# Streaming-encoder trunk, float32 on one core: in the last quarter of both MLPs, the weights of the last product split ahead of those of the last but one

## Chip, core and metric

The kernel runs on one core of a Trainium2 chip. Its time is what the device needs for one execution, in microseconds, as the median over several executions. Before the change three executions took 1416.71, 1417.35 and 1418.65 us, so the median is 1417.35 us.

## What is computed

The trunk has two residual layers over 512 tokens of width 1024. The first mixes tokens with a Mamba-2 scan, the second with stick-breaking attention. Each mixer is followed by a LayerNorm, then by an MLP with a squared ReLU, then by another LayerNorm:

```python
D_MODEL, SEQ, DEPTH, D_FF = 1024, 512, 2, 4096
DEEPNORM_ALPHA = (2 * DEPTH) ** 0.25

def squared_relu_mlp(h, w1, w2):
    return jnp.square(jax.nn.relu(h @ w1)) @ w2
...
    for layer in range(DEPTH):
        if layer < N_A_LAYERS:
            mix = mamba2_mixer(h, ...)
        else:
            if layer == N_A_LAYERS:
                k, v = shared_kv(h, sb_w_k, sb_w_v)
            mix = stick_breaking_attention(h, sb_w_q[j], k, v, sb_w_o[j])
        h = layer_norm(DEEPNORM_ALPHA * h + mix, ln_mix_g[layer], ln_mix_b[layer])
        h = layer_norm(DEEPNORM_ALPHA * h + squared_relu_mlp(h, mlp_w1[layer], mlp_w2[layer]),
                       ln_mlp_g[layer], ln_mlp_b[layer])
    return h
```

Only the two MLPs, and what follows each of them, concern the change. After the first MLP come its LayerNorm and the projections to v, q and k. After the second come its LayerNorm and the output.

## The kernel before

**Precision.** Every operand of a matrix product is split in two: a high part (a cast of the value, on ScalarE, named `wh` for weights) and a low part (the value less its high part, mostly on VectorE, named `wl`). A product is then three matmuls (`mm3`, lines 208 to 210): high with high, and the two mixed ones.

**Weights.** All weights come through one list, `stream`, in pieces of 128x1024 (512 KB). `emit_w` (from line 150) handles the next piece: SyncE's queue loads it into one of two `raw` buffers (`wr`), ScalarE casts the high part (line 191), VectorE subtracts for the low part (line 193). The split pair takes a buffer from a ring of six in the MLPs (four in `wp`, two in the MLP's own pool). `load_w` hands a piece to its product and keeps splitting up to four pieces ahead (`prefetch`). Since there are two `raw` buffers, the load of a piece can begin only when the low part of the piece two places before it has been formed.

**The MLP's second matrix.** It is applied in four quarters of the hidden width, each as a 2x2 block product with seven products instead of eight, P1 to P7. Four of them need a sum or difference of weight blocks, kept in buffers `rawa` and `rawc` (two of each, one for each half `s` of a piece pair): `t1` leaves its sum in `rawa`, `t2` in `rawc`, and `t3` and `t4` read `rawc`. The order of the products is P1, P5, P6, P4, P7, P2, P3, each with two pieces of weights and 24 matmuls of 512 columns. They gather in four pairs of PSUM banks: X (P1, P6, P7), Y (P5, then P3), Z (P4), V (P2). VectorE adds a finished pair onto the residual `v`: line 435 for a plain add, line 432 for an add that also leaves the row sums that the norm needs (`ln_sums`). "Row 2" is token tiles 0 and 1, "row 1" is token tiles 2 and 3.

**The last quarter.** P7 finishes row 2, which can then be normalised: sums (line 343), squares on ScalarE (346), 1/sqrt on GpSimd (348 to 354), shift (359) and scale (365) on VectorE. P2 (banks V, left half of the columns) and P3 (banks Y, right half) finish row 1. In the first MLP the normed rows are transposed on TensorE into banks `ln_b` (396), copied out as `ln_hh` (399) and `ln_hl` (400), and used by the projections `pv`, `pq` and `pk`, first for row 2 and then for row 1. In the second MLP the normed rows are written out (367).

**What sets the order.** The code is recorded in program order, and a scheduler then places the instructions of each engine by its own estimate. `issue_after` (in the first MLP for P2, P3 and what follows, in `by_token` for the second) only bounds where something may be placed. So the order on an engine follows from when the scheduler expects the operands, the split weights among them. Once the program is built, each engine runs its instructions in that fixed order.

Of the kernel before, what the change touches and what calls it, by code (L numbers as in the profile page):

```python
# [12 lines left out]
F32R = mybir.dt.float32r  # L13
# [4 lines left out]
P = 128  # L18
# [17 lines left out]
def trunk(ctx: ExitStack, tc: tile.TileContext, io):  # L36
    nc = tc.nc
# [16 lines left out]
    def f(x):  # L54
        return x.bitcast(F32)
# [28 lines left out]
    stream = []  # L84
    marks = []
# [56 lines left out]
    ready = []  # L142
# [2 lines left out]
    alt = {}  # L145
    upto = [len(stream)]
    sums = {}
    depth = [2]

    def emit_w():  # L150
        i = len(ready)
        pool, e = extra[:2]
        if i >= extra[4]:
            pool = None
        use = pool is not None and e > 0 and i % (4 + e) >= 4
        px, b = (pool, e) if use else (wp, 4)
        sfx = "x" if use else ""
        rb = extra[2]

        def fetch(src, tag=None):  # L160
            if tag is not None:
                raw = pool.tile([P, 1024], F32, tag=tag, name=f"{tag}{i}", bufs=2)
            elif pool is not None and i % (2 + rb) >= 2:
                raw = pool.tile([P, 1024], F32, tag="rawx", name=f"wr{i}", bufs=rb)
            else:
                raw = wp.tile([P, 1024], F32, tag="raw", name=f"wr{i}", bufs=2)
            nc.sync.dma_start(raw, src)
            return raw

        item = stream[i]  # L170
        if not isinstance(item, tuple):
            raw = fetch(item)
        elif item[0] == "t1":
            raw = sums[item[1]] = fetch(item[2], "rawa")
            nc.vector.tensor_sub(raw, raw, fetch(item[3]))
        elif item[0] == "t2":
            raw = fetch(item[2], "rawc")
            nc.vector.tensor_sub(raw, raw, sums[item[1]])
            sums[item[1]] = raw
        else:  # L180
            raw = fetch(item[2])
            if item[0] == "t3":
                nc.vector.tensor_sub(raw, sums[item[1]], raw)
            else:
                nc.vector.tensor_sub(raw, raw, sums[item[1]])
        if i in alt:
            hi, lo = alt[i](i)
        else:
            hi = px.tile([P, 1024], F32R, tag="hi" + sfx, name=f"wh{i}", bufs=b)
            lo = px.tile([P, 1024], F32R, tag="lo" + sfx, name=f"wl{i}", bufs=b)  # L190
        nc.scalar.copy(hi, raw)  # L191
        eng = nc.gpsimd if extra[3] and i % 4 == 1 else nc.vector
        eng.tensor_sub(lo, raw, f(hi))  # L193
        ready.append((hi, lo))

    def prefetch(n):
        while len(ready) < min(upto[0], taken[0] + n):
            emit_w()
# [1104 lines left out]
```

## Time and profile before

| what | value |
|---|---|
| median of three executions | 1417.35 us |
| the profiled execution's own time | 1416.35 us |
| its span | 1414.2 us |
| mean granted TensorE clock | 0.997 |
| busy TensorE matmul / weight load | 1389.0 us / 1197.0 us |
| busy VectorE / ScalarE / GpSimd | 1076.8 / 783.8 / 221.8 us |
| HBM read / written | 159.65 MB / 2.10 MB |

The span is the stretch from the first to the last event in the trace; 2.15 us of the profiled execution's time lie outside it. A row of the timeline gives the start, the duration, the engine, the line and operation, what is written and read, and in brackets how long the engine was idle before and what ended that. Matmuls overlap in the pipeline: one of 512 columns is shown with 0.39 us and the next begins 0.227 us later. Neighbouring rows on VectorE overlap a little too, so the cost of an instruction in a row of busy ones is the distance between starts.

### The profile page before, as it was taken

The page shows a single profiled execution, that of the slowest core. Times are in us where ns is not written, and L with a number is a line of the kernel's source. Part 1 is how long each engine was busy: PE and PEld are TensorE (multiplying, and loading weights), DVE is VectorE, ACT ScalarE, POOL GpSimd, SP SyncE. Part 2 cuts the span into 40 slices and gives each one's busy share as a digit, 9 for nine tenths or more (in the row PEclk, how much of TensorE's full clock was granted, in tenths as well). Part 3 has the DMA queues.
Part 4 walks back from the last instruction along what each step waited for, and adds up shares of the span by engine and source line. Part 5 has one row for each costly group of instructions (what it writes and reads, how often), then busy time and mean ns, then how long its engine had stood idle before and what let it go on. Part 6 is the DMA issues. An engine that isn't in the chain of part 4 may idle for free.

```text
span 1414.2 us, 19327 instructions
## 1 busy us (share of the span) xinstructions
PE 1389.0 (98%) x7414; PEld 1197.0 (85%) x7414; DVE 1076.8 (76%) x1530; ACT 783.8 (55%) x1264; POOL 221.8 (16%) x249
## 2 busy tenths in 40 slices
PE   9999999999999999999999999999999999999996
PEld 6898897889997988888888799899889888888885
DVE  5798898368887596785859868787877966858588
ACT  5556575246653363635445568898853636454463
POOL 2344555034443100000000200000000000000001
PEclk9999999999999999999999999999999999999998
DMA  5223222222223345455453521121223455454533
GB/s 186 76 77 133 70 66 75 89 81 70 74 65 107 115 162 169 159 162 166 134 169 116 163 90 47 44 75 46 75 90 120 134 179 164 149 168 139 168 116 123
DMA packets 46699, 162.99 MB, mean 115 GB/s; under 512 B 5520, under 2 KB 5776, under 8 KB 46608
## 3 DMA queue, kind: packets, MB, share of 16 engines
q1 hardware_dynamic: 44016, 157.44, 34.9%
q10 hardware_dynamic: 2592, 4.33, 1.0%
q8 instruction: 58, 0.95, 0.3%
q14 instruction: 33, 0.27, 0.1%
HBM read 159.65 MB, written 2.10 MB: 114 GB/s over the span
## 4 chain that ended last, share of the span: by engine, by line
PE 87%; DVE 7%; ACT 2%; DMA 2%; issue 1%; POOL 1%; ACTq 0%; SPq 0%; DVEq 0%; POOLq 0%
PE f L209 8%; PE f L210 8%; PE f L208 8%; PE X L210 3%; PE X L208 3%; PE X L209 3%; PE pz L208 2%; PE pz L210 2%; PE pz L209 2%; PE px L208 2%; PE px L209 2%; PE px L210 2%; PE Y L210 2%; PE Y L209 2%; PE Y L208 2%; PE z L1141 1%
## 5 line engine op out<-in xcount | busy, mean ns | idle before, releaser
L191 ACT CAST wh<-wr 128x1024 fp32r<-128x1024 f32 x235 | 246.6, 1050 | 326.1 <-DMA wr<-w 159.1
L193 DVE TENSOR_TENSOR wl<-wr,wh 128x1024 fp32r<-128x1024 f32 x218 | 268.6, 1233 | 181.6 <-ACT wh L191 180.8
L210 PE MATMUL f<-ln_hh,wl 128*128 128x512 f32 (+1 forms) x544 | 201.2, 371 | 0.0
L209 PE MATMUL f<-ln_hl,wh 128*128 128x512 f32 (+1 forms) x544 | 201.2, 371 | 0.0
L208 PE MATMUL f<-ln_hh,wh 128*128 128x512 f32 (+1 forms) x544 | 200.3, 371 | 0.0
L210 PEld LDWEIGHTS f<-ln_hh,wl 128*128 128x128 f32 x544 | 102.4, 188 | 17.8 <-DVE wl L193 0.4
L209 PEld LDWEIGHTS f<-ln_hl,wh 128*128 128x128 f32 x544 | 102.4, 188 | 17.7 <-DVE ln_hl L400 0.2
L208 PEld LDWEIGHTS f<-ln_hh,wh 128*128 128x128 f32 x544 | 102.0, 188 | 17.4
L348 POOL TENSOR_TENSOR ln_rs<-ln_sums 128x1 f32<-128x1 f32 (+1 forms) x6 | 3.1, 513 | 632.6 <-ACT lnr L346 632.6
L208 PE MATMUL X<-wh,hP 128*128 128x512 f32 x192 | 74.7, 389 | 0.0
L209 PE MATMUL X<-wl,hP 128*128 128x512 f32 x192 | 74.7, 389 | 0.0
L210 PE MATMUL X<-wh,l 128*128 128x512 f32 x192 | 74.0, 389 | 0.0
L210 PE MATMUL pz<-wh,x_l 128*128 128x256 f32 x256 | 72.7, 284 | 0.0
L209 PE MATMUL pz<-wl,x_h 128*128 128x256 f32 x256 | 72.6, 284 | 0.0
L208 PE MATMUL pz<-wh,x_h 128*128 128x256 f32 x256 | 72.4, 283 | 0.0
L461 ACT CAST hP<-r 128x512 fp32r<-128x512 f32 x80 | 48.1, 620 | 32.0 <-DVE r L473 31.1
L193 POOL TENSOR_TENSOR wl<-wr,wh 128x1024 fp32r<-128x1024 f32 x17 | 42.6, 2504 | 92.3 <-ACT wh L191 92.0
L208 PE MATMUL px<-x_h,wh 128*128 128x512 f32 x128 | 50.8, 397 | 0.0
L209 PE MATMUL px<-x_l,wh 128*128 128x512 f32 x128 | 50.3, 393 | 0.0
L210 PE MATMUL px<-x_h,wl 128*128 128x512 f32 x128 | 50.2, 392 | 0.0
L209 PE MATMUL Y<-wl,hP 128*128 128x512 f32 x128 | 49.8, 389 | 0.0
L209 PEld LDWEIGHTS pz<-wl,x_h 128*128 128x128 f32 x256 | 48.8, 190 | 0.9
(1365 smaller groups left out, 3923.0 us busy)
## 6 DMA issues: line engine op xcount, KB each, us to landing
wr<-w SPq DMA_DIRECT2D x160, 512.0 KB, 3.6
wr<-w_bc SPq DMA_DIRECT2D x16, 512.0 KB, 3.5
wr<-w_x SPq DMA_DIRECT2D x16, 512.0 KB, 3.5
wr<-w_z SPq DMA_DIRECT2D x16, 512.0 KB, 3.5
wr<-w_so SPq DMA_DIRECT2D x16, 512.0 KB, 3.5
rawa<-w SPq DMA_DIRECT2D x16, 512.0 KB, 3.7
rawc<-w SPq DMA_DIRECT2D x16, 512.0 KB, 4.4
wr<-w_qk SPq DMA_DIRECT2D x16, 512.0 KB, 3.5
```

Source lines behind the costliest of these rows:

```text
L191: nc.scalar.copy(hi, raw)
L193: eng.tensor_sub(lo, raw, f(hi))
L208: nc.tensor.matmul(out, a[0], b[0], start=start, stop=False, skip_group_check=skip)
L209: nc.tensor.matmul(out, a[0], b[1], start=False, stop=False, skip_group_check=skip)
L210: return nc.tensor.matmul(out, a[1], b[0], start=False, stop=stop, skip_group_check=skip)
L348: nc.gpsimd.tensor_add(rs, self.sq[:, t0:t1, 0], self.sq[:, t0:t1, 1])
L461: nc.scalar.copy(h, src)
L1141: w_end[0] = nc.tensor.matmul(zj, ntri_ge, x, start=False, stop=i == 1, skip_group_check=True).ins
```

## The change

Where the second piece of P7 has been split (`i in last_t3`, five places before the end of each MLP's stream), the two pieces of P3 (places `i + 3` and `i + 4`) are now loaded and split at once, ahead of the two of P2. Their high and low parts go to four tiles with the tags `rawc` and `rawa`, whose buffers held the sums of weight blocks. When `emit_w` later comes to those places, it takes the kept pair and issues nothing. No instruction is added or left out.

```diff
+    spare = {}
+    last_t3 = (marks[1] - 5, marks[3] - 5)
...
     def emit_w():
         i = len(ready)
+        if i in spare:
+            ready.append(spare[i])
+            return
...
         eng.tensor_sub(lo, raw, f(hi))
         ready.append((hi, lo))
+        if i in last_t3:
+            for n, tag in ((i + 3, "rawc"), (i + 4, "rawa")):
+                hi, lo = (pool.tile([P, 1024], F32R, tag=tag, name=f"{tag}{n}{j}", bufs=2) for j in "hl")
+                raw = fetch(stream[n])
+                nc.scalar.copy(hi, raw)
+                nc.vector.tensor_sub(lo, raw, f(hi))
+                spare[n] = (hi, lo)
```

The lines of the changed file are 12 higher below this place (208 becomes 220, 432 becomes 444). The order on the engines moves at three places. In the rows, V with a number is one half of P2's bank pair, Y with a number one half of P3's, `ln_b` with a number one bank of transposes.

VectorE at the end of the first MLP, before, from the sums of row 2 to the first low part of the transposed rows:

```order
L343 TENSOR_SCALAR ln_sums<-ln_sums 128x1
L193 TENSOR_TENSOR wl_7366<-wr_7363,wh_7365 128x1024
L359 SCALAR_TENSOR_TENSOR v<-v,ln_sums,lnr_7308 128x1024
L432 SCALAR_TENSOR_TENSOR v,ln_sums<-v,V_7391 128x512
L432 SCALAR_TENSOR_TENSOR v,ln_sums<-v,V_7392 128x512
L359 SCALAR_TENSOR_TENSOR v<-v,ln_sums,lnr_7308 128x1024
L365 SCALAR_TENSOR_TENSOR v<-v,ln_rs,lnr_7308 128x1024 x2
L193 TENSOR_TENSOR wl_7409<-wr_7406,wh_7408 128x1024
L432 SCALAR_TENSOR_TENSOR v,ln_sums<-v,Y_7226 128x512
L432 SCALAR_TENSOR_TENSOR v,ln_sums<-v,Y_7227 128x512
L193 TENSOR_TENSOR wl_7497<-wr_7494,wh_7496 128x1024
L400 TENSOR_TENSOR ln_hl<-ln_b_7452,ln_hh 128x2x256
```

The same stretch of VectorE in the changed kernel:

```order
L355 TENSOR_SCALAR ln_sums<-ln_sums 128x1
L198 TENSOR_TENSOR wl_7346<-wr_7343,wh_7345 128x1024
L371 SCALAR_TENSOR_TENSOR v<-v,ln_sums,lnr_7320 128x1024 x2
L377 SCALAR_TENSOR_TENSOR v<-v,ln_rs,lnr_7320 128x1024 x2
L198 TENSOR_TENSOR wl_7409<-wr_7406,wh_7408 128x1024
L444 SCALAR_TENSOR_TENSOR v,ln_sums<-v,Y_7226 128x512
L444 SCALAR_TENSOR_TENSOR v,ln_sums<-v,Y_7227 128x512
L198 TENSOR_TENSOR wl_7497<-wr_7494,wh_7496 128x1024
L444 SCALAR_TENSOR_TENSOR v,ln_sums<-v,V_7391 128x512
L444 SCALAR_TENSOR_TENSOR v,ln_sums<-v,V_7392 128x512
L412 TENSOR_TENSOR ln_hl<-ln_b_7452,ln_hh 128x2x256
```

The two adds of V stood between the two shifts of row 2. They now stand behind the second weight piece of `pv` (`wl_7497`), directly ahead of the first `ln_hl`.

TensorE near the end of the second MLP, before, where the first matmuls of P2 stand (`wh_12836` is P2's first piece, `wh_12809` P7's second, X_12703 one half of P7's banks):

```order
L208 MATMUL X_12703<-wh_12809,hP_12386 128x512
L208 MATMUL V_12936<-wh_12836,hP_12387 128x512
L208 MATMUL V_12937<-wh_12836,hP_12387 128x512
L209 MATMUL X_12703<-wl_12810,hP_12386 128x512
L210 MATMUL X_12703<-wh_12809,l_12382 128x512
```

In the changed kernel the first matmuls of P2 stand here (`rawa271h` and `rawa271l` are P3's second piece, `wh_12848` is P2's first):

```order
L222 MATMUL Y_12745<-rawc270h,lP_12390 128x512
L220 MATMUL Y_12745<-rawa271h,hP_12389 128x512
L220 MATMUL V_12936<-wh_12848,hP_12387 128x512
L220 MATMUL V_12937<-wh_12848,hP_12387 128x512
L221 MATMUL Y_12745<-rawa271l,hP_12389 128x512
```

P2 stood inside P7 and ran ahead of the whole of P3. Now P3 stands first, and P2 begins in the middle of P3's first half (Y_12745) and ends last.

VectorE at the end of the program, before, from P3's adds to the last scales:

```order
L432 SCALAR_TENSOR_TENSOR v,ln_sums<-v,Y_12745 128x512
L365 SCALAR_TENSOR_TENSOR v<-v,ln_rs,lnr_12827 128x512
L343 TENSOR_SCALAR ln_sums<-ln_sums 128x1
L432 SCALAR_TENSOR_TENSOR v,ln_sums<-v,Y_12746 128x512
L343 TENSOR_SCALAR ln_sums<-ln_sums 128x1
L359 SCALAR_TENSOR_TENSOR v<-v,ln_sums,lnr_12827 128x512 x3
L365 SCALAR_TENSOR_TENSOR v<-v,ln_rs,lnr_12827 128x512 x2
```

The same stretch in the changed kernel:

```order
L377 SCALAR_TENSOR_TENSOR v<-v,ln_rs,lnr_12839 128x512 x3
L444 SCALAR_TENSOR_TENSOR v,ln_sums<-v,Y_12746 128x512
L444 SCALAR_TENSOR_TENSOR v,ln_sums<-v,V_12936 128x512
L444 SCALAR_TENSOR_TENSOR v,ln_sums<-v,V_12937 128x512
L355 TENSOR_SCALAR ln_sums<-ln_sums 128x1 x2
L371 SCALAR_TENSOR_TENSOR v<-v,ln_sums,lnr_12839 128x512 x3
L377 SCALAR_TENSOR_TENSOR v<-v,ln_rs,lnr_12839 128x512 x2
```

Before, the sums of token tile 2 stood ahead of the last add, and those of tile 3 behind it. Now the adds of V come last, and the sums of both tiles stand behind the last add.

## Prediction

> **What bounds the kernel now.** I read the page first, then the windows around both places that change, then the chain of waits and the timelines there. The page:
>
> ```profile
> span 1414.2 us, 19327 instructions
> PE 1389.0 (98%) x7414; PEld 1197.0 (85%) x7414; DVE 1076.8 (76%) x1530; ACT 783.8 (55%) x1264; POOL 221.8 (16%) x249
> PE 87%; DVE 7%; ACT 2%; DMA 2%; issue 1%; POOL 1%; ACTq 0%; SPq 0%; DVEq 0%; POOLq 0%
> ```
>
> TensorE carries 87% of the chain. A change in the order of two products can pay only where TensorE waits near them. The windows (length, then busy time and count for PE, PEld, DVE, ACT, POOL, granted clock, DMA) cover the end of the first MLP, the seam to `pv`, the first projections, and the end of the second MLP:
>
> ```profile
> 780.00:799.30 19.30, 19.30 (x88) 15.90 (x86) 16.04 (x27) 9.37 (x14) 3.47 (x8) 1.00 0.52 163
> 799.30:805.00 5.70, 3.45 (x23) 2.34 (x21) 5.70 (x10) 2.65 (x5) 2.22 (x3) 1.00 0.36 104
> 805.00:816.00 11.00, 11.00 (x95) 11.00 (x93) 9.37 (x12) 5.39 (x12) 2.19 (x3) 1.00 0.44 138
> 1375.00:1403.00 28.00, 28.00 (x125) 22.98 (x123) 24.23 (x39) 9.75 (x15) 3.43 (x6) 1.00 0.34 115
> ```
>
> In P7, P2 and P3 of both MLPs TensorE has no gap: 125 matmuls in 28.00 us are 0.224 us each, which is the pitch of a running pipeline. So the weights of P2 and P3 are in time today, and splitting some of them earlier removes no wait. TensorE waits only in the seam, 5.70 - 3.45 = 2.25 us, and after its last matmul. The chain of waits through the seam (start, duration, what):
>
> ```profile
> 797.71 1.69 DVE v L365 x2
> 799.40 0.72 issue
> 800.12 1.30 DVE wl L193
> 801.42 1.21 DVE v L432 x4
> 802.64 1.14 DVE wl L193
> 803.77 0.61 DVE ln_hl L400
> 804.43 0.39 PE pv L210
> ```
>
> Here VectorE is the bound. It scales row 2, forms a weight piece of `pv`, adds the two halves of Y, forms the second piece, and then the first `ln_hl`. `pv` goes on 0.05 us after that. Whatever is put into this row of VectorE moves `pv` by its own length.
>
> **The change, part by part.** The loads, casts and subtractions are the same in number and size. Only which piece uses which of four successive slots changes: P3's two pieces take the first two, P2's the last two. On SyncE's queue four loads of equal size swap places, so nothing is passed that is longer or shorter. I cost the transfers and casts at nothing, as the cover is the slack until TensorE needs a piece. It is smallest in the second MLP, for P2's first piece in the third slot. The rows are of ScalarE's cast in that slot, VectorE's low parts of the second, third and fourth slot, and the last matmul of P7:
>
> ```profile
> 1391.77 1.05 ACT L191 CAST wh<-wr 128x1024 fp32r<-128x1024 f32 x1 [1.66 <-DMA wr<-w]
> 1390.14 1.22 DVE L193 TENSOR_TENSOR wl<-wr,wh 128x1024 fp32r<-128x1024 f32 x1 [1.68 <-ACT wh L191]
> 1392.85 1.23 DVE L193 TENSOR_TENSOR wl<-wr,wh 128x1024 fp32r<-128x1024 f32 x1 [0.27 <-ACT wh L191]
> 1396.12 1.21 DVE L193 TENSOR_TENSOR wl<-wr,wh 128x1024 fp32r<-128x1024 f32 x1
> 1392.34 0.39 PE L210 MATMUL X<-wh,l 128*128 128x512 f32 x1
> ```
>
> The third slot's high part is there at 1391.77 + 1.05 = 1392.82. In the new order one matmul fewer stands inside P7, so P7's last starts one pitch earlier, at 1392.11. Six of P3 follow, and P2's first starts at 1392.11 + 7 x 0.227 = 1393.70: 0.88 us of slack. The second slot's low part now has an add of X ahead of it and may end up to one add later (0.6 us, half the pair of adds in the chain above), near 1392.0. It is used at about 1394.2. It frees a `raw` buffer, so the fourth slot slips with it, from 1397.33 to about 1397.9 at most. P2's second piece needs that low part only ten matmuls before the end, near 1400.7. All have cover. If it were gone, each late us would cost one us.
>
> The kept tiles lie where sums of weights lay. Those were last read in forming P7's pieces, which were split just before, so no new wait is in front of the cast. The banks Y were emptied of P5 long before P3 enters them. Both cost nothing.
>
> **First term, the seam.** V is now finished with Y, when TensorE leaves the MLP, and the scheduler put its two adds behind the second `pv` piece, ahead of `ln_hl`. Today they stand here, between the shifts (the second row is the next instruction of another kind):
>
> ```profile
> 794.35 0.68 DVE L432 SCALAR_TENSOR_TENSOR v<-v,V 128x512 f32<-128x512 f32 x1
> 795.56 1.28 DVE L359 SCALAR_TENSOR_TENSOR v<-v,ln_sums,lnr 128x1024 f32<-128x1024 f32 x1
> 797.71 2.49 DVE L365 SCALAR_TENSOR_TENSOR v<-v,ln_rs,lnr 128x1024 f32<-128x1024 f32 x2 [0.86 <-POOL ln_rs L354]
> ```
>
> The two adds with the reading of their sums take 795.56 - 794.35 = 1.21 us. Where they stand they cost nothing: behind them VectorE idles 0.86 us until GpSimd has 1/sqrt. That instant depends on the sums and squares of row 2, which stay put, so the scale still begins at 797.71, and VectorE idles 0.86 + 1.21 us instead. Behind it stand scale, piece, Y, piece, V, `ln_hl`: the first `ln_hl` begins 1.21 us later than 803.77, and `pv` goes on at 804.43 + 1.21 = 805.64. What is queued behind the adds: the four `ln_hl`, the sums of row 1, the low parts for `pq` and `pk`. First term: **+1.2 us**, from 0.9 to 1.6 (one `ln_hl` step of 0.6 us either half hidden or half added).
>
> Behind that, row 1 must be normed before TensorE runs out of work of row 2. The rows are of ScalarE's third square with the last read of sums, the two scales of row 1, and TensorE's first transposes of row 1:
>
> ```profile
> 808.46 0.72 ACT L346 ACTIVATE lnr<-v,ln_sums 128x512 f32<-128x512 f32 x1
> 809.94 0.18 ACT L346 ACTIVATION_READ_ACCUMULATOR lnr<-v,ln_sums 128x1 f32 x1
> 812.60 2.48 DVE L365 SCALAR_TENSOR_TENSOR v<-v,ln_rs,lnr 128x1024 f32<-128x1024 f32 x2 [0.83 <-POOL ln_rs L354]
> 815.56 0.60 PE L396 MATMUL ln_b<-ident,v 128*128 128x128 f32 x4
> ```
>
> The squares that ended at 810.12 were spread between casts. All four now stand behind the last cast. That cast keeps its place and ends where the square above begins, at 808.46. The last two squares took 810.12 - 808.46 = 1.66 us, so four end near 811.8, 1.7 us later. GpSimd's part, 812.60 - 810.12 = 2.5 us, puts the scale at about 814.3, and tile 3 is done near 816.8. TensorE asks for tile 2 at 815.56 + 1.2 + 0.12 = 816.9 and for tile 3 some 0.5 us after that. This is just hidden, so no cost, with about 0.6 us of cover.
>
> **Second term, the end.** VectorE is also the bound after TensorE's last matmul:
>
> ```profile
> 1402.77 0.39 PE L210 MATMUL Y<-wh,lP 128*128 128x512 f32 x1
> 1403.72 0.21 DVE L343 TENSOR_SCALAR ln_sums<-ln_sums 128x1 f32<-128x1 f32 x1
> 1403.84 0.68 DVE L432 SCALAR_TENSOR_TENSOR v<-v,Y 128x512 f32<-128x512 f32 x1
> 1404.56 0.21 DVE L343 TENSOR_SCALAR ln_sums<-ln_sums 128x1 f32<-128x1 f32 x1
> 1404.02 0.72 ACT L346 ACTIVATE lnr<-v,ln_sums 128x512 f32<-128x512 f32 x1 [5.55 <-DVE ln_sums L343]
> ```
>
> VectorE's work up to the last add is the same and stays without a gap, so the last add still ends about 1404.5, though it is now V's. V is ready at 1403.16, which is early enough. But the sums of tile 2 stood ahead of the last add, at 1403.72, and now stand behind it, at 1404.56. ScalarE's squares, which the rest hangs on (1/sqrt, scales, output), start 0.84 us later. Second term: **+0.8 us**, from 0.3 (if VectorE gets through 0.5 us sooner) to 1.4 (if the fourth slot's slip of 0.6 us shows).
>
> **Sum.** 1.2 + 0.8 = +2.0 us, or 0.14%. Against the profiled execution that is 1416.35 + 2.0 = 1418.4. That execution is 1.0 us below the median of the three shown. As a median I forecast 1417.35 + 2.0 = **1419.4 us**. The terms alone reach from +1.2 to +3.0. About 0.2% (2.8 us) is what a measurement of this kernel can tell from no change, so this counts as no change, but near the edge.
>
> **Rivals.**
>
> *A, slower: the clock falls in the seam.* After the last matmul the granted clock shows when it is taken away (two of the one-us windows):
>
> ```profile
> 1406.00:1407.00 1.00, 0.00 (x0) 0.00 (x0) 0.93 (x2) 0.97 (x3) 0.88 (x2) 0.97 0.00 0
> 1407.00:1408.00 1.00, 0.00 (x0) 0.00 (x0) 0.57 (x2) 0.37 (x2) 0.91 (x3) 0.50 0.00 0
> ```
>
> It halves at 1406.94, which is 3.8 us after the last matmul ended (1403.16). In the seam TensorE does this now (last matmul of the MLP, first of `pv`, last eight transposes of row 2):
>
> ```profile
> 798.93 0.40 PE L210 MATMUL Y<-wh,lP 128*128 128x512 f32 x1
> 801.47 0.39 PE L208 MATMUL pv<-wh,ln_hh 128*128 128x256 f32 x1 [0.35 <-ACT ln_hh L399]
> 802.08 1.26 PE L396 MATMUL ln_b<-ident,v 128*128 128x128 f32 x8
> ```
>
> The last product ends at 799.33, `pv` puts in two matmuls at 801.47, and goes on at 804.43, with transposes between, at a clock of 1.00. Afterwards the two matmuls stand behind the transposes that wait for the first add of Y, near 802.6: pauses of 3.3 and 2.5 us if transposes don't count, under 2.3 us if they do. From 3.8 us without activity this decides. If full speed takes as long to come back as it took to go, half of 3.8 us is lost: 1.9 us, so 1421.3 in all. [...] Chance 0.10.
>
> *B, slower: row 1 or a weight piece comes late.* The cover is 0.6 us for tile 3's scale and 0.88 us for P2's first piece. If either chain is late by 1 us beyond its cover, TensorE stands that long: 2.0 + 1.0 = +3.0, 1420.4. For it: the squares in one block, and GpSimd, whose part took 2.5 us there. Against: both covers are worked out from rows and positive. Chance 0.12.
>
> *C: the seam's term is given back.* If a later wait of TensorE on something that does not move (a transfer) absorbs it, +0.8 remains, 1418.2. Against: weights after the seam are loaded when TensorE frees buffers, and move with it. Chance 0.14.
>
> *D, faster: weights were the bound after all.* The chain of waits gives DMA 2%. If earlier splitting took one `wl` step of 1.2 us from the end, the sum would be 1416.2. Against it: 28.00 busy of 28.00. Chance 0.05.
>
> **How the numbers follow.** The forecast holds 0.59. The three times shown lie within 1.9 us of each other, so a measured difference can be off by about 1 us. The range takes in the terms' lower end less that (1417.35 + 1.2 - 1.0, a little lower for C and D) and A at its top: 1416.9 to 1421.9. Slower by over 0.2%: A 0.10, B about 0.09, and of the forecast and C 0.08 for the terms' upper end and measurement, 0.27. Faster by over 0.2% needs D and a lucky measurement: 0.04. The rest, 0.69, is no change.
>
> **What would show it.** Right: no gap in TensorE up to the end of P2, `pv` resuming about 6.3 us after the last product (5.1 before), V's adds directly ahead of the first `ln_hl`, the last squares starting about 1.7 us after TensorE's last matmul ended (0.86 before), clock 1.00 in the seam. Wrong: a wait of `ln_b` on the scale of row 1 over 0.3 us, a matmul waiting for a weight piece, a clock below 1, or a seam no longer than before.

## The result and the profile after

The changed kernel takes 1421.26 us (median of eight executions, 1419.97 to 1422.56) and the kernel before 1416.93 us (eight executions beside them, 1416.51 to 1418.77). The ratio is 1.0028, with a 95% interval of 1.0017 to 1.0039. So the change costs about 4 us and makes the kernel slower by 0.28%. The forecast was 1419.4 us, with no change (within 0.2%) as the likeliest class, at 0.69. The time fell inside the range of 1416.9 to 1421.9 us, but the loss is twice the 2.0 us of the sum.

The profiled execution took 1419.97 us, its span 1418.0 us instead of 1414.2 us. Its 3.8 us can be followed along TensorE. First the head of the page:

```profile
span 1418.0 us, 19323 instructions
PE 1390.6 (98%) x7414; PEld 1199.4 (85%) x7414; DVE 1075.8 (76%) x1530; ACT 784.8 (55%) x1264; POOL 222.2 (16%) x249
```

The number of matmuls is the same, and yet they are busy for 1.6 us longer, although no product grew. The windows show where (columns as in the prediction). The first and the last hold the ends of the two MLPs, the others the seam:

```profile
776.00:799.50 23.50, 23.50 (x106) 19.40 (x105) 18.17 (x26) 10.37 (x15) 3.60 (x8) 1.00 0.44 134
1375.00:1405.70 30.70, 30.70 (x136) 25.10 (x134) 26.40 (x42) 10.10 (x15) 4.08 (x6) 1.00 0.36 117
...
799.00:805.00 6.00, 2.97 (x21) 2.13 (x19) 6.00 (x12) 2.25 (x4) 2.45 (x4) 1.00 0.66 182
805.00:806.00 1.00, 0.37 (x1) 0.37 (x2) 1.00 (x2) 0.42 (x1) 0.00 (x0) 0.65 0.67 164
806.00:807.00 1.00, 1.00 (x6) 1.00 (x6) 1.00 (x3) 0.63 (x1) 0.00 (x0) 0.50 0.69 279
...
808.00:809.00 1.00, 1.00 (x8) 1.00 (x8) 0.74 (x1) 0.77 (x1) 0.00 (x0) 0.65 0.00 0
```

Up to the end of each MLP TensorE has no gap, as before. In the seam the granted clock drops to one half. A window with a mean of 0.65 has been at half speed for 0.35 / 0.5 = 0.70 us, so the clock falls at 805.30 and is back at 808.70, after 3.40 us. Before, the clock was 1.00 there. TensorE's rows in the seam, from the last matmul of the MLP, and the first transposes of row 1:

```profile
799.16 0.39 PE L222 MATMUL V<-wh,lP 128*128 128x512 f32 x1
...
802.07 0.66 PE L408 MATMUL ln_b<-ident,v 128*128 128x128 f32 x4 [0.96 <-DVE v L444]
802.48 0.36 PE L220 MATMUL pv<-wh,ln_hh 128*128 128x256 f32 x1
...
802.80 0.60 PE L408 MATMUL ln_b<-ident,v 128*128 128x128 f32 x4
805.63 0.58 PE L222 MATMUL pv<-wh,ln_hl 128*128 128x256 f32 x1 [2.23 <-DVE ln_hl L412]
...
818.23 0.60 PE L408 MATMUL ln_b<-ident,v 128*128 128x128 f32 x4
```

`pv` goes on at 805.63 (804.43 before), and the reason stands on VectorE: V's two adds are directly ahead of the first `ln_hl`.

```profile
797.69 2.49 DVE L377 SCALAR_TENSOR_TENSOR v<-v,ln_rs,lnr 128x1024 f32<-128x1024 f32 x2 [0.87 <-POOL ln_rs L366]
...
803.68 0.67 DVE L444 SCALAR_TENSOR_TENSOR v<-v,V 128x512 f32<-128x512 f32 x1
...
804.29 0.68 DVE L444 SCALAR_TENSOR_TENSOR v<-v,V 128x512 f32<-128x512 f32 x1
...
804.90 2.47 DVE L412 TENSOR_TENSOR ln_hl<-ln_b,ln_hh 128x512 fp32r<-128x512 f32 x4
```

The first transposes of row 1 come 818.23 - 815.56 = 2.67 us later than before. Of this, 1.20 us is the later `pv`, 0.12 us is one matmul more that now stands ahead of them, and the remaining 1.35 us is the clock. The same sum from `pv` to these transposes gives 1.50 us for the two other profiles with a fall in this place (12.75 us in e1 and e8 below, 11.13 us before), and 0.01 us for the filled kernel, which kept its clock (11.26 us in e3). The transposes are ready in time: the row shows no wait. VectorE starts to scale row 1 before that:

```profile
815.02 2.48 DVE L377 SCALAR_TENSOR_TENSOR v<-v,ln_rs,lnr 128x1024 f32<-128x1024 f32 x2 [0.83 <-POOL ln_rs L366]
```

From there to the last matmul nothing more is lost: it ends at 1405.71 instead of 1403.16, which is 1.20 + 1.35 us. Behind it stands the rest. TensorE's last matmul, VectorE's rows around it, and ScalarE's first square of row 1:

```profile
1405.32 0.39 PE L222 MATMUL V<-wh,lP 128*128 128x512 f32 x1
```

```profile
1402.34 0.75 DVE L377 SCALAR_TENSOR_TENSOR v<-v,ln_rs,lnr 128x512 f32<-128x512 f32 x1 [0.44 <-POOL ln_rs L366]
...
1406.27 0.68 DVE L444 SCALAR_TENSOR_TENSOR v<-v,V 128x512 f32<-128x512 f32 x1
...
1406.88 0.68 DVE L444 SCALAR_TENSOR_TENSOR v<-v,V 128x512 f32<-128x512 f32 x1
...
1407.48 0.33 DVE L355 TENSOR_SCALAR ln_sums<-ln_sums 128x1 f32<-128x1 f32 x2
```

```profile
1407.78 0.72 ACT L358 ACTIVATE lnr<-v,ln_sums 128x512 f32<-128x512 f32 x1 [6.41 <-DVE ln_sums L355]
```

From the last matmul's end to the end of the span it is now 1418.0 - 1405.71 = 12.29 us; before it was 1414.2 - 1403.16 = 11.04 us. The first square starts 2.07 us after the last matmul, where it was 0.86 before and 1.7 were forecast. These 1.21 us have two parts. From the start of the last add to the square it is now 1407.78 - 1406.88 = 0.90 us, and was 1404.02 - 1403.84 = 0.18 us: 0.72 us for the place of the sums. And the last add itself starts 1.17 us after the last matmul instead of 0.68: 0.49 us. Ahead of it VectorE waits 0.44 us for GpSimd, which it did not do there before. So the 3.8 us of the span are 1.20 (seam), 1.35 (clock) and 1.25 (end).

### The profile page after: what moved, and what is told of

It is laid out like the page before. It is cut to its first block, busy times and chain, and to the rows that moved or that the text cites. A ratio compares the mean times of both kernels' runs of the same rounds, so it can differ in the third digit from the quotient of the medians.

```text
span 1418.0 us, 19323 instructions
## 1 busy us (share of the span) xinstructions
PE 1390.6 (98%) x7414; PEld 1199.4 (85%) x7414; DVE 1075.8 (76%) x1530; ACT 784.8 (55%) x1264; POOL 222.2 (16%) x249
## 5 line engine op out<-in xcount | busy, mean ns | idle before, releaser
L196 ACT CAST wh<-wr 128x1024 fp32r<-128x1024 f32 x231 | 242.5, 1050 | 320.0 <-DMA wr<-w 155.2
L198 DVE TENSOR_TENSOR wl<-wr,wh 128x1024 fp32r<-128x1024 f32 x214 | 263.3, 1232 | 176.2 <-ACT wh L196 175.2
L220 PEld LDWEIGHTS pz<-wh,x_h 128*128 128x128 f32 x256 | 48.7, 190 | 0.8
```

Source lines behind the costliest of these rows:

```text
L220: nc.tensor.matmul(out, a[0], b[0], start=start, stop=False, skip_group_check=skip)
```

## Experiments

The theory after the result: three costs add up, namely VectorE's longer row in the seam, a clock that is taken away because the pause there is longer, and VectorE's new order at the end. The main rival is that the weights that were moved come late somewhere, and that the clock is an accident of one execution. Two further questions are what of the end is the place of the sums, and what is the slip of the fourth weight slot, which the prediction had as the upper end of its second term.

Differences of medians below are against the kernel before as it ran on the same chip beside each kernel: 1417.03 us (33 executions) for e1 to e4, 1417.14 us (31) for e5 to e8, 1417.13 us (19) for e9 and e10. The ratios are those on record and not the quotients of these medians. Their intervals reach about 0.0009 to either side, which is 1.3 us, so no single time below is sharper than that. "The stretch at the end" is from the end of TensorE's last matmul to the end of the span.

### The change in one MLP only

The first kernel (e1) has the change in the first MLP only, the second (e2) in the second only:

```diff
-    last_t3 = (marks[1] - 5, marks[3] - 5)
+    last_t3 = (marks[1] - 5,)
```

```diff
-    last_t3 = (marks[1] - 5, marks[3] - 5)
+    last_t3 = (marks[3] - 5,)
```

> The change made at the end of the first MLP alone, so only the seam to pv can move. Theory 1: V's adds hold back the first low part by 1.2 us, and in the longer, emptier pause the granted clock halves for some 3.4 us, which costs 1.3 us more: pv resumes 1.2 us later than before, and TensorE leaves the first projections 2.5 us later; time +1.2 to +2.6 us, depending on how often the clock falls. Theory 2: the slow matmuls come from the moved weights (their new buffers or transfers), not from the pause: the same time here. This run gives the seam's share; both theories want the end of the program unchanged against before.

> The change made at the end of the second MLP alone, so only the end can move. Both theories: the seam is as before, clock 1.00 there, TensorE's last matmul ends when it did, and the stretch behind it is 0.8 us (as predicted) to 1.25 us (as the profile of the changed kernel has it) longer; time +0.8 to +1.3 us. If the shares of the two halves don't add up to the whole, something else is at work.

The first MLP alone takes 1419.5 us (1.0013, interval 1.0004 to 1.0022), the second alone 1418.55 us (1.0010, interval 1.0001 to 1.0019): +2.5 and +1.5 us. Their sum of 4.0 us is close to the whole; by the two ratios it is 3.3 us. So each half costs. In the first one the clock falls again, and its rows say more than those of the changed kernel. Three one-us windows, then the row in which TensorE goes on:

```profile
806.00:807.00 1.00, 0.95 (x8) 0.95 (x9) 1.00 (x2) 0.44 (x1) 0.00 (x0) 1.00 0.89 352
807.00:808.00 1.00, 1.00 (x8) 1.00 (x7) 1.00 (x5) 0.00 (x0) 0.00 (x0) 0.57 0.21 82
...
810.00:811.00 1.00, 1.00 (x9) 1.00 (x8) 0.66 (x2) 0.97 (x3) 0.00 (x0) 0.72 0.90 131
```

```profile
806.05 0.38 PE L222 MATMUL pv<-wh,ln_hl 128*128 128x256 f32 x1 [2.23 <-DVE ln_hl L412]
```

The clock falls at 807.14, when TensorE has been at work again for 1.1 us, and comes back at 810.56, 3.42 us later. The longest gap before it was 2.23 us. So here the clock was not taken away inside the gap but 1.1 us after it had ended, and the fall lasted as long as the changed kernel's (3.40 us).

With the second MLP alone the clock in the seam is 1.00, and its stretch at the end is 1415.3 - 1403.57 = 11.73 us, +0.69 instead of +1.25, although the order of the instructions is the same there. This spread is taken up below.

### The seam filled, and V's adds moved without any weights

One kernel (e3) is the changed one with eight matmuls of ones, whose result is not used, in the pause behind row 2's last transposes. The other (e4) is the kernel before, with nothing of the change in it but the place of V's two adds in the first MLP:

```diff
...
+                    fill = psum("mm", [P, 4, P], "fill")
+                    with tc.issue_after(nxt.turned.ins):
+                        for _ in range(8):
+                            nc.tensor.matmul(fill, ones_r, ones_r.unsqueeze(1).to_broadcast([P, 4, P]),
+                                             start=True, stop=True)
```

```diff
-                    add(1, 0, Z, True)
...
                         end = add(1, 1, Y, True)
+                    with tc.issue_after(end.ins):
+                        add(1, 0, Z, True)
```

> The changed kernel with 8 matmuls of ones, 1.8 us, put into TensorE's pause behind the last transposes of row 2; their product is used by nobody. Theory 1 (the clock falls because the pause is empty): the clock stays 1.00, pv still resumes about 1.2 us later than before, TensorE leaves the first projections 1.2 to 1.5 us later instead of 2.5, time 1.0 to 1.3 us below the changed kernel, that is about +2.5 us against before. Theory 2 (the moved weights): pv's first matmuls are as slow as in the changed kernel, time as the changed kernel's or more.

> The kernel before, its weights in their old order, with V's two adds at the end of the first MLP moved behind Y's adds, as the changed kernel has them. Theory 1: pv resumes 1.2 us later, and as the pause is the same as the changed kernel's the clock can fall here too: +1.2 us without a fall, +2.5 with one. Theory 2: +1.2 us and the clock at 1.00 in every case, since no weight moves.

Filled, the kernel takes 1419.04 us (1.0013, interval 1.0004 to 1.0022), +2.0 us and so 2 us less than the changed kernel, although it does more work. (1.0 to 1.3 us less were expected; the difference is within the intervals.) Its rows in the seam:

```profile
803.61 2.10 PE L572 MATMUL fill<-ones_r 128*128 128x512 f32 x8
...
806.16 0.39 PE L222 MATMUL pv<-wh,ln_hl 128*128 128x256 f32 x1 [0.22 <-DVE ln_hl L413]
```

The clock is 1.00 throughout the seam. `pv` goes on no sooner. What came back is not VectorE's row, but the clock.

With V's adds alone moved, the time is 1419.87 us (1.0019, interval 1.0010 to 1.0028), +2.8 us. All weights stay in their old order there. The rival of the late weights falls: the loss of the first MLP is there without them. `pv` goes on 7.94 us after the start of row 2's scale in this kernel, in the changed one (805.63 - 797.69) as well, and 6.72 us after it before (804.43 - 797.71):

```profile
797.61 2.49 DVE L365 SCALAR_TENSOR_TENSOR v<-v,ln_rs,lnr 128x1024 f32<-128x1024 f32 x2 [0.86 <-POOL ln_rs L354]
...
805.55 0.39 PE L210 MATMUL pv<-wh,ln_hl 128*128 128x256 f32 x1 [2.23 <-DVE ln_hl L400]
```

The profiled execution of this kernel kept its clock in the seam, though its gap is the same 2.23 us, and lost it at another place (3.42 us from 240.68 us on, behind a gap of 1.00 us that the kernel before has too).

Why the same pause can end either way shows in where the clock changes. Within one execution these places lie on a grid of 3.413 us, as long as one fall (3.40 and 3.42 us above): in the changed kernel there are 600.74 us, or 176 such steps, from the clock's return at 808.71 to its fall at 1409.45, at the end of the program. In e1 and e8 the same distance is 600.74 us too, in this kernel and e6 it is 1163.94 us or 341 steps, and in e7 597.34 us or 175. Counted along this grid from the falls, these windows cover the pause, first one of the kernel before, then one of the changed kernel, then two of the present one (V's adds alone):

```profile
799.36:802.78 3.42, 2.25 (x15) 1.44 (x14) 3.42 (x7) 1.08 (x3) 2.16 (x3) 1.00 0.16 23
```

```profile
801.88:805.29 3.41, 1.33 (x10) 1.10 (x10) 3.41 (x10) 1.19 (x3) 0.00 (x0) 1.00 0.74 201
```

```profile
800.48:803.89 3.41, 1.88 (x16) 1.41 (x13) 3.41 (x10) 2.19 (x4) 1.00 (x1) 1.00 0.42 123
803.89:807.30 3.41, 1.75 (x14) 1.75 (x15) 3.41 (x7) 2.06 (x5) 0.00 (x0) 1.00 0.47 149
```

In the changed kernel one window takes in most of the pause, TensorE is busy for 1.33 us of it, and the clock falls at its end. The windows ahead of the falls of e1 and of the changed kernel's repetition (e8) are busy for 1.18 and 1.19 us. With V's adds alone the grid cuts the same pause in two, 1.88 and 1.75 us, and the clock stays. So in these profiles it went with the place of the grid whether the pause cost clock, and one profile can't say what it costs on average. Transposes count as work in these traces: the filled kernel's window from 799.70 to 803.11 us is busy for 1.80 us, 1.77 us of it with transposes, and keeps the clock, while e1's window ahead of its fall holds 1.09 us of other matmuls.

Busy time is not the whole measure, since two falls near 241 us (this kernel and e6) come behind windows with 2.4 us, filled with short matmuls that are shown with 0.27 us and follow each other after 0.11 us. An estimate counts columns instead (512 of them as 0.227 us, the distance of such matmuls in these traces, and a transpose double, which was chosen after the event because it fits). By it the windows ahead of the falls of the changed kernel, e1, e7, e8 and this kernel hold 0.95 to 1.27 us of work, and each other window at full clock up to the last matmul holds 1.46 us or more in the kernel before and 1.52 us or more in the changed one.

### The changed kernel once more

> This is the changed kernel once more, for more executions beside the others of this row. If the longer pause in the first projection costs clock in most executions, its mean granted clock is 0.996 or lower in at least half of them (the kernel before: 0.997 or higher in about three quarters), and those are 1 to 1.5 us longer than the others. The ratio to the kernel before is 1.0024 (1.2 us seam, 1.25 us end, and about 1 us of clock on average). If the clock has no part in it, the ratio is 1.0017 and the clocks are spread as those of the kernel before.

This (e8) takes 1421.01 us, 1.0026 with an interval of 1.0016 to 1.0035. All nine executions have a mean clock of 0.996 or lower; of the kernel before, 22 of 83 do. The profiled execution loses the clock in the seam again, from 805.94 to 809.36:

```profile
805.00:806.00 1.00, 0.23 (x1) 0.23 (x2) 1.00 (x4) 0.65 (x1) 0.00 (x0) 0.97 0.76 225
...
809.00:810.00 1.00, 1.00 (x9) 1.00 (x8) 0.77 (x1) 0.97 (x4) 0.00 (x0) 0.82 0.33 37
```

Each execution comes with its mean granted clock, in steps of 0.001. One fall of 3.4 us at half speed takes 0.5 x 3.4 / 1417 = 0.0012 off it. So the mean over the executions counts the falls, with one correction that follows the table:

| kernel | pause in the seam | mean clock (executions) | median against before |
|---|---|---|---|
| before, all runs of the study | as before | 0.9969 (83) | |
| second MLP only | as before | 0.9965 (11) | +1.5 us |
| second MLP only, other ends (e5, e6, e9, e10) | as before | 0.9966 (42) | +0.3 to +1.2 us |
| changed, pause filled | longer, filled | 0.9967 (11) | +2.0 us |
| first MLP only | longer | 0.9960 (11) | +2.5 us |
| V's adds late | longer | 0.9953 (11) | +2.8 us |
| pause moved (e7, last section) | moved | 0.9959 (11) | +1.7 us |
| changed, both series | longer | 0.9954 (17) | +4.3 and +3.9 us |

The kernel before has a fall in some executions as well: in 83 executions those at 0.997 have a median of 1416.97 us, and those at 0.996 of 1418.11 us. The changed kernel is 0.0015 lower on average, but not all of that is falls. The mean also takes in the end of the program, where no matmul is left and the clock is at one half: 1414.2 - 1406.94 = 7.3 us of the profile before, 1418.0 - 1409.45 = 8.5 us of the changed one. The five kernels with the change in the second MLP only have the old pause and a longer end, and stand at 0.9966 (53 executions). Against them the changed kernel is 0.0012 lower, which is one fall more in each execution, or 1.35 to 1.5 us. In the profiles, three of the four executions with the longer pause unfilled lost the clock in the seam, and none of the six with the old pause did, nor the filled one. (Two of the six, e5 and e6, lost it once elsewhere, at 17.07 and 241.30 us.) That the longer pause takes the clock in these kernels is therefore shown. Whether all of the 1.4 us or so is lost in the seam is not: the mean clock is on record for the whole of an execution, not for a place.

### The end: the sums, the slip and GpSimd

Four kernels have the change in the second MLP only. In the first (e5), V's last add stands behind the sums of tile 2:

```diff
...
+                        with tc.issue_after(nxt.summed.ins if j else end_x.ins):
+                            add(1, 0, Z, True, (j,))
...
```

> This has the change in the second MLP only, with V's add of tile 3 moved behind the reading of tile 2's sums, so that VectorE's order after the last product is Y, V, sums of tile 2, V, sums of tile 3. If the end's term is the place of the sums (they stood ahead of the last add and now stand behind it), the first square starts about one add and its reading (0.6 to 0.8 us) sooner, and the stretch from TensorE's last matmul to the end of the span falls from 12.3 us to about 11.5 us. If the end's term is only that VectorE gets to its adds late (the slip of the fourth weight slot), the stretch stays within 0.2 us of 12.3 us. Against the kernel before: +0.4 us where the first holds, +1.3 us where the second does.

VectorE's last add with the sums ahead of it, and ScalarE's first square:

```profile
1405.60 0.69 DVE L445 SCALAR_TENSOR_TENSOR v<-v,V 128x512 f32<-128x512 f32 x1
...
1406.33 0.21 DVE L355 TENSOR_SCALAR ln_sums<-ln_sums 128x1 f32<-128x1 f32 x1
1406.46 0.68 DVE L445 SCALAR_TENSOR_TENSOR v<-v,V 128x512 f32<-128x512 f32 x1
```

```profile
1406.64 0.72 ACT L358 ACTIVATE lnr<-v,ln_sums 128x512 f32<-128x512 f32 x1 [6.02 <-DVE ln_sums L355]
```

The square starts 0.18 us after the start of the last add again, so the 0.72 us are back. Part of it is paid on VectorE: the last add starts 0.86 us after the one ahead of it instead of 0.61, as the sums now stand between. That leaves 0.47 us. The stretch at the end is 1416.8 - 1405.05 = 11.75 us, 0.54 less than in the changed kernel (about 11.5 us were expected). The time is 1418.35 us (1.0003, interval 0.9994 to 1.0012).

The second kernel (e6) takes the slip away: X's adds of tile 0 stand behind the low part of P3's second piece.

```diff
...
-                nc.vector.tensor_sub(lo, raw, f(hi))
+                split[0] = nc.vector.tensor_sub(lo, raw, f(hi))
...
+                        with tc.issue_after(split[0].ins) if layer == 1 else nullcontext():
+                            add(2, 0, X, True, (j,))
```

> This has the change in the second MLP only, with the add of X's first tile moved behind the low part of P3's second piece, so that the buffer is freed as early as before and the fourth slot's cast doesn't slip. If the part of the end's loss beyond 0.84 us comes from that slip (GpSimd's row of 1/sqrt late by it, and VectorE waiting for GpSimd by 0.44 us after the last add), the cast of the fourth slot starts near 1397.3 us instead of 1397.9 us, VectorE's wait for GpSimd in the tail is under 0.1 us, and the stretch from the last matmul to the end of the span falls from 12.3 us to about 11.9 us. If the slip has no part in it, the stretch stays at 12.3 us. One add of tile 0 then stands elsewhere among the adds of the last products, which is to cost nothing.

The cast of the fourth slot does start earlier: 8.30 us before the end of the last matmul, where it was 7.80 in the changed kernel and 8.15 before. But VectorE still waits 0.44 us for GpSimd, and the stretch is 1415.7 - 1403.60 = 12.10 us. The time is 1418.05 us (1.0007, interval 0.9998 to 1.0016). So the slip does not cause this wait, and without it the stretch is only 0.19 us shorter than in the changed kernel. What causes the wait, GpSimd's rows show, first before, then in this kernel, with VectorE's rows beside them:

```profile
1396.85 0.54 POOL L348 TENSOR_TENSOR ln_rs<-ln_sums 128x1 f32<-128x1 f32 x1 [316.93 <-ACT lnr L346]
1397.47 0.57 POOL L349 TENSOR_SCALAR ln_rs<-ln_rs 128x1 f32<-128x1 f32 x1
1398.13 0.55 POOL L354 TENSOR_TENSOR ln_rs<-ln_rs,mhalf 128x1 f32<-128x1 f32 x1
```

```profile
1397.12 1.21 POOL L361 TENSOR_TENSOR ln_rs<-ln_sums 128x1 f32<-128x1 f32 x1 [316.77 <-ACT lnr L359]
1398.42 0.57 POOL L362 TENSOR_SCALAR ln_rs<-ln_rs 128x1 f32<-128x1 f32 x1
1399.08 0.94 POOL L367 TENSOR_TENSOR ln_rs<-ln_rs,mhalf 128x1 f32<-128x1 f32 x1
```

```profile
1397.07 1.21 DVE L199 TENSOR_TENSOR wl<-wr,wh 128x1024 fp32r<-128x1024 f32 x1
1398.20 1.41 DVE L372 SCALAR_TENSOR_TENSOR v<-v,ln_sums,lnr 128x512 f32<-128x512 f32 x2
1400.05 0.75 DVE L378 SCALAR_TENSOR_TENSOR v<-v,ln_rs,lnr 128x512 f32<-128x512 f32 x1 [0.44 <-POOL ln_rs L367]
```

The same step of one column takes 0.54 us in one place and 1.21 us in another. The longer one began 0.05 us after the subtraction `wl` and ended at 1398.33, which is 0.13 us after VectorE's next instruction had begun. Its next step ends at 1398.99, just behind the start of the second shift. The third meets no such place and ends at 1400.02, with VectorE idle since 1399.61. In the kernel before the three steps end at 1397.39, 1398.04 and 1398.68, which is 0.14, 0.12 and 0.16 us after VectorE began a shift (1397.25), an add of V (1397.92) and the other shift (1398.52). So a step of GpSimd beside a busy VectorE ends, in these rows, where VectorE goes from one instruction to the next. Before, the add of V between the two shifts was one of these three places, so VectorE had work until 1/sqrt was there. Now Y's add stands ahead of `wl` instead, and only two shifts are left.

This was tested by putting Y's add between the two shifts, alone (e9), and together with e5's lines (e10):

```diff
...
+                        with nullcontext() if j else tc.issue_after(nxt.shifted[1].ins):
                             add(1, 1, Y, True, (j,))
```

> This has the change in the second MLP only, with the add of Y's first tile moved from ahead of the last weight piece's low part to a place between the two shifts behind it, where an add of V stands in the kernel before. If VectorE's 0.44 us of waiting for GpSimd comes from the order around that low part (GpSimd's short steps end only 0.1 us behind the next start on VectorE, and the add gives them one more such place while VectorE has work), the wait is gone or under 0.1 us, VectorE's last add starts 0.4 us sooner after TensorE's last matmul, and the stretch from the last matmul to the end of the span is 11.8 to 11.9 us instead of 12.29 us. If the wait comes from the slip of the fourth weight slot, it stays at 0.44 us and the stretch at 12.1 to 12.3 us.

> This is the kernel with V's last add behind the sums of tile 2, and with the add of Y's first tile between the shifts as well. If the end's +1.25 us is the place of the sums (0.5 to 0.8 us) and the wait for GpSimd (0.44 us), the two add up, and the stretch from the last matmul to the end is 11.2 to 11.4 us (11.04 us in the kernel before); against the kernel before the time is then within 0.5 us. If they are one and the same cost, the stretch stays at 11.7 us.

In e9 the wait is gone, with the fourth slot's cast as late as in the changed kernel (7.82 us before the last matmul's end). It is gone in e10 too, and stands at 0.44 us in all six profiles that have the new end without this edit. GpSimd's third step, then VectorE's rows:

```profile
1398.20 0.55 POOL L367 TENSOR_TENSOR ln_rs<-ln_rs,mhalf 128x1 f32<-128x1 f32 x1
```

```profile
1397.98 0.68 DVE L445 SCALAR_TENSOR_TENSOR v<-v,Y 128x512 f32<-128x512 f32 x1
...
1398.59 0.75 DVE L372 SCALAR_TENSOR_TENSOR v<-v,ln_sums,lnr 128x512 f32<-128x512 f32 x1
```

The last add starts 0.87 us after the last matmul's end, 1.17 us in the changed kernel. The stretch is 1414.9 - 1402.91 = 11.99 us, a little over the 11.8 to 11.9 us expected. With both, it is 1416.5 - 1405.05 = 11.45 us, 0.84 us below 12.29, as much as the gains of 0.54 and 0.30 us together. It is still 0.4 us above the kernel before, and expected were 11.2 to 11.4 us. In e10 VectorE waits 0.88 us for the fourth slot's cast, which it does not in the kernel before, so later loads are the likely rest, but no run singles that out. The times are 1417.45 us (1.0004, interval 0.9995 to 1.0014) and 1417.64 us (1.0007, interval 0.9997 to 1.0017). Neither can be told from the kernel before, and neither beats it.

The stretch also varies from execution to execution of one order of instructions. The old end gave 11.04, 11.18, 11.16 and 11.25 us in four profiles (before, e1, e4, e7). The new end gave 12.29, 12.34, 11.81 and 11.73 us (changed, changed again, e3, e2). The mean difference is 0.9 us. Taken apart, only one piece of the stretch varies:

| profiles | last add starts after the last matmul's end | first square starts after the last add | cast of the third slot before the last matmul's end |
|---|---|---|---|
| old end (before, e1, e4, e7) | 0.7 to 0.9 us | 0.2 us | 11.2 to 11.4 us |
| new end (changed, e8) | 1.2 us | 0.9 us | 11.3 us |
| new end (e2, e3) | 0.7 us | 0.9 us | 12.1 us |
| without the slip (e6) | 1.0 us | 0.9 us | 11.5 us |
| Y between the shifts (e9) | 0.9 us | 0.9 us | 11.2 us |
| sums between (e5) | 1.4 us | 0.2 us | 11.3 us |
| both (e10) | 1.1 us | 0.2 us | 12.3 us |

From the square to the end it is 10.2 us in all twelve. So the place of the sums costs its 0.7 us in every profile. The start of the last add, with the same order and the same wait of 0.44 us, differs by 0.5 us, and it is early where the third slot's cast is early. On average over four profiles it is 0.93 us with the new end and 0.79 us with the old one. Gains of 0.2 to 0.3 us in one profile are therefore read safely only between profiles with the cast in the same place. By that, e9's 0.30 us stands, one profile against the changed kernel's two. That the two gains add up is not shown: e10 has the early cast, and against e2 and e3 it is only about 0.3 us shorter.

### A shorter seam

A last kernel (e7) has nothing of the change. It turns the idea round and lets VectorE form the first low parts between the two weight pieces, ahead of Y's adds:

```diff
-                pt = psum("bg", [P, 2, w], f"{nm}_b{mm}{t0}")
+                own = self.sums and t0 == 0 and mm >= 2
+                pt = psum("mm" if own else "bg", [P, 2, w], f"{nm}_b{mm}{t0}")
...
+                    with tc.issue_after(nxt.low[2].ins):
+                        add(1, 1, Y, True)
...
-                    with tc.issue_after(end.ins):
+                    with tc.issue_after(nxt.low[1].ins):
```

> This is the kernel before without the change, with a shorter seam: the last eight transposes of row 2 go to banks of the MLP's sums, and VectorE forms the first low parts of the norm between the two weight pieces of the first projection instead of behind both and behind Y's adds. If VectorE's row ahead of the first low part sets when the first projection goes on, it goes on near 802.0 us instead of 804.43 us, with the clock at 1.00 there, and TensorE's last matmul ends 0.3 to 1.4 us sooner than 1403.16 us (less than the 2.4 us, as the later low parts or the norm of row 1 may then be waited for). The rival, that the seam's length is set by what stands behind it (the norm of row 1): the last matmul ends within 0.2 us of 1403.16 us and the time is that of the kernel before.

It takes 1418.85 us, +1.7 us (1.0011, interval 1.0003 to 1.0020). `pv` goes on at 801.88, as expected, but TensorE then runs out of weights:

```profile
801.88 0.39 PE L210 MATMUL pv<-wh,ln_hl 128*128 128x256 f32 x1 [0.18 <-DVE ln_hl L402]
...
807.48 0.58 PE L208 MATMUL pq<-ln_hh,wh 128*128 128x256 f32 x1 [2.30 <-ACT wh L191]
```

```profile
808.00:813.00 5.00, 5.00 (x26) 5.00 (x25) 4.51 (x5) 3.44 (x9) 1.33 (x2) 0.50 0.56 158
```

The high part of `pq`'s first piece, not the norm of row 1, is what comes next, and ScalarE's cast of it waits for its load:

```profile
806.38 1.04 ACT L191 CAST wh<-wr 128x1024 fp32r<-128x1024 f32 x1 [3.82 <-DMA wr<-w_qk]
```

In that pause the clock falls for 6.82 us, twice 3.41 us. The last matmul ends at 1406.55, 3.4 us later than before, where 0.3 to 1.4 us sooner were expected. Moving the pause gained nothing and cost clock.

## Why the prediction was right and wrong

**First term, the seam: right.** +1.2 us was forecast by the two adds, `pv` at 805.64. It came at 805.63, and with V's adds alone moved the distance to the scale grew by the same 1.22 us. The pause came out at 6.1 us instead of 6.3, because the last product ended 0.2 us later.

**Weights and row 1: right.** TensorE has no gap up to the end of P2 in either MLP, and row 1's transposes wait for nothing. Row 1's scale began at 815.0 instead of 814.3, so the cover was thinner than the 0.6 us forecast. In the filled kernel, whose clock stayed, the scale ends at 815.34 + 2.48 = 817.82 and the transposes of tile 3 start at 817.98 without a wait: 0.16 us were left.

**Second term, the end: right in kind, mis-sized at its upper end, which was laid to the wrong cause.** +0.8 us was forecast for the place of the sums. The place of the sums measured 0.72 us. The step that failed here is "the last add still ends about 1404.5": as measured from the last matmul it starts 0.49 us later in the changed kernel. That made +1.25 us of the term in the profiled execution. The mean of four is 0.9 us, and in it the last add is only 0.14 us later, so on average the step nearly held. The upper end of 1.4 us was laid to the slip of the fourth slot. Without the slip the wait of 0.44 us for GpSimd stayed (e6); with the slip, but with Y's add between the shifts, it went (e9). What the prediction missed is that the new order took from GpSimd one change of instruction on VectorE, and that the last add moves by 0.5 us between executions, together with the cast of the third slot.

**The clock: the step that failed.** Rival A had the right event, and nearly the right price (1.9 us forecast, 1.35 in the profile, about 1.4 on average), at a chance of 0.10. It failed in its condition: "From 3.8 us without activity this decides." That figure was taken from the end of the program in one profile. In the twelve profiles the clock falls there 2.1 us (e3) to 5.1 us (e1) after the last matmul has ended. In the seam the longest gap is 2.23 us, and in e1 the clock fell 1.1 us after work had resumed. What goes with a fall in the traces is how little TensorE does in one window of 3.41 us, transposes included (1.33 us of work shown ahead of the fall in the changed kernel, 2.25 us in the kernel before), and not its longest gap: in e4 the clock stayed after 2.23 us and fell after 1.00 us. By either reading of the transposes the prediction's pauses (3.3 us, or under 2.3 us) were below its 3.8 us, and yet the clock fell. Where exactly the limit lies stays open but for the estimate above.

**The sum.** 1.2 (seam), 0.9 (end) and 1.4 (clock) make 3.5 us, against +4.3 and +3.9 us in the two series; the rest is within the intervals. The forecast left out the third term. The time lies in the range only because the range had been drawn to take in rival A at its top, at a chance of 0.10. Rivals B, C and D have nothing in the runs that speaks for them.

## What to carry to other kernels

When the instructions that a waiting engine must pass before it can go on become more, count the length of the pause twice: once as the wait itself (1.20 us here), and once as a chance that TensorE's clock falls behind it (about 1.4 us here), which showed in the mean granted clock over many executions (0.9954 against 0.9966 with the old pause) and not in each profile (e4 kept its clock in the seam). Sums that start a chain on another engine should stand ahead of adds that do not feed them (0.72 us here). In these traces GpSimd's short steps were priced by where VectorE changes its instruction (0.54 or 1.21 us for the same step): look at what stands on VectorE beside them before moving a step away.

## What the runs showed of the hardware

Ahead of the end of the program a fall of the clock to one half lasted 3.4 us in five profiles (changed, changed again, e1, e4, e6) and 6.82 us, twice that, in one (e7). Within each of these executions the changes lie on a grid of 3.413 us (175 to 341 steps between the clock's return and its fall at the end), whose place differs from execution to execution: in the seam the falls began at 805.30, 805.94 and 807.14 us (changed, changed again, e1). One fall began inside a gap of 2.30 us (e7), another 1.1 us after work had resumed (e1), and transposes counted as work (1.77 of 1.80 us in a window of e3 that kept the clock). A step of one column on GpSimd took 0.54 us in one place (before) and 1.21 us in another (e6, beside a subtraction on VectorE), and ended 0.14 and 0.13 us after VectorE's next instruction had begun.
